# Low parts of the projection weights: an accumulating DMA in place of GpSimd's subtraction

## The chip, the cores and the metric

The kernel runs on one core of one Trainium2 chip. The metric is the device time of one execution in microseconds. Engines are named as the profile names them: PE (TensorE matmuls; PEld its weight loads), DVE (VectorE), ACT (ScalarE), POOL (GpSimd), SP (SyncE, which here only issues DMAs).

## What is computed

One block of a hybrid network over 2048 tokens of width 1024: a normalised and modulated input `h`, one large projection into 5960 columns, an RWKV-7 branch (a scan with state), an attention branch over the 256 best keys of each query, chosen by an index score, and a gated merge.

```python
h = rms_norm(x, norm_g[l]) * (1.0 + scale[:, None, :]) + shift[:, None, :]
p = h @ w_in[l]
...
y_a = rwkv7_branch(pr, pk, pv, pwd, pad_, w0[l], w2[l], a0[l], a2[l], k_k[l], k_a[l],
                   r_k[l], lnx_g[l], lnx_b[l])
y_b = dsa_branch(q, ckv, qi, ki, wi, kv_norm_g[l], w_uk[l], w_uv[l], rel_bias)
br_a = (y_a * jax.nn.silu(z_a)) @ w_pa[l]
br_b = (y_b * jax.nn.silu(z_b)) @ w_pb[l]
merged = jax.nn.sigmoid(g_a) * br_a + jax.nn.sigmoid(g_b) * br_b
x = x + gate[:, None, :] * (merged @ w_o[l])
```

The change is in `p = h @ w_in`.

## The kernel before

The projection is a GEMM in float32r with both operands split in two: a rounded high part (float32r) and what the rounding left, the low part. Each product takes three matmuls: weight high by `h` high, weight high by `h` low, weight low by `h` high, in this order for each of 8 slices of the contraction (L250 and L251). A *unit* is one block of 128 output columns for 512 tokens: 24 matmuls of 512 columns, or 48 of 256 (`self.cut`) in the second half. The tokens are four blocks of 512. First `gemm_index` makes five column blocks for all four token blocks; then `gemm_half` makes 42 column blocks for token blocks 0 and 1, and the same 42 for blocks 2 and 3. Between the halves, `h` of blocks 2 and 3 is loaded from DRAM into the same buffers. At this turn of the halves (the last two column blocks of the first, the first two of the second) a token block serves two column blocks in turn.

The weights of one column block are made in `weights_` (L228 to L238), 89 times: SP loads 512 KB into `wraw`, of which there is one buffer (`bufs=1`); ACT casts it into `whi`; POOL subtracts the two into `wlo`. `whi` and `wlo` have two buffers each. So the cast for a block waits for the load and for the matmuls of the block before last, and the next load waits for the subtraction. The first block has 72 columns; the rest of its 128 is set to zero.

After a unit, ACT and DVE take its result from PSUM (`evacuate`: tile `eo`, four buffers) and SP stores it. Around the GEMM run the selection (`select`: PE's index scores `ixs`, ACT's `re`, DVE's `sc`) and the RWKV passes. The order of instructions on each engine is fixed when the kernel is built: a scheduler plays the program through and takes what is ready, by priority; `weights` and `evacuate` run as `urgent`, ahead of all else. Each engine then takes its instructions in that order, SP's and POOL's DMAs too, and one that waits holds up those behind it.

Of the kernel before, what the change touches and what calls it, by code (L numbers as in the profile page):

```python
# [24 lines left out]
FT = mybir.dt.float32  # L25
FR = mybir.dt.float32r
BF = mybir.dt.bfloat16
I32 = mybir.dt.int32
AF = mybir.ActivationFunctionType
OP = mybir.AluOpType  # L30
# [10 lines left out]
TOPK = 256  # L41
# [4 lines left out]
# first columns of the projections  # L46
# [5 lines left out]
class Block:  # L52
# [19 lines left out]
    def move(self, dst, src, q=None):  # L72
        """a DMA of float32r words as they are"""
        f = [a.bitcast(FT) if a.dtype == FR else a for a in (dst, src)]
        return (q or self.nc.sync).dma_start(f[0], f[1])
# [4 lines left out]
    # ---------------------------------------------------------------- constants  # L80
    def consts(self):
# [6 lines left out]
        # scratch in DRAM  # L88
# [23 lines left out]
    # ---------------------------------------------------------------- start: modulation, norm, h^T  # L112
    def start(self):
# [59 lines left out]
        # the last third of the modulation is for the end  # L173
# [9 lines left out]
        # bias by distance; beyond the last bucket's start it is constant and drops out of the softmax  # L183
# [12 lines left out]
    def ada(self, w, cT, j, ahead):  # L196
        """a third of the modulation, partial sums by partition"""
# [15 lines left out]
    # ---------------------------------------------------------------- the projection GEMM  # L213
    @contextmanager
    def urgent(self):
        """what frees or feeds the tensor engine goes before all else"""
# [10 lines left out]
    def weights_(self, c0, n):  # L227
# [5 lines left out]
        if n < 128:  # L233
            nc.gpsimd.memset(hi.bitcast(FT), 0.0)
            nc.gpsimd.memset(lo.bitcast(FT), 0.0)
        nc.scalar.copy(hi[:, :, :n], raw[:, :, :n])  # L236
        nc.gpsimd.tensor_tensor(lo[:, :, :n], raw[:, :, :n], hi[:, :, :n].bitcast(FT), op=OP.subtract)  # L237
# [17 lines left out]
    def split_out(self, p, scale=None, rows=128):  # L255
        """FR hi and lo of a PSUM tile."""
# [44 lines left out]
    def gemm_half(self, tbs, kinds):  # L301
# [13 lines left out]
        # at the turn of the halves, a block of tokens serves two columns at a time  # L315
# [55 lines left out]
    # ---------------------------------------------------------------- index scores and the selection  # L371
    def select(self):
        """For each query the mask of its TOPK best keys (ties go to the lower index).

        A threshold is sought by the secant method on the count of scores at or above it, until the count is
        at most eight short of TOPK; the missing ones are then the largest below the threshold. Where the
        search has not ended so, a branch finds the TOPK-th largest value bit by bit.
        """
# [3 lines left out]
        with ExitStack() as ctx:  # L382
# [15 lines left out]
            for grp in self.groups:  # L398
# [9 lines left out]
                for g, qb in enumerate(grp):  # L408
# [20 lines left out]
                    # a first guess from mean and mean deviation of the keys that all rows see  # L429
# [10 lines left out]
                for it in range(self.passes):  # L440
                    if it:
                        # next threshold: a step of nothing once the count is near enough
# [15 lines left out]
                    for g, qb in enumerate(grp):  # L458
                        n = 128 * (qb + 1)
                        tg, cg = t[:, g:g + 1], cnt[:, g:g + 1]  # L460
                        if qb in self.on_act and it < self.passes - 1:
                            # with Sign a score equal to the threshold counts half: good enough to go on
# [5 lines left out]
                # rows that found their threshold  # L468
# [29 lines left out]
    def select_bits(self, grp, sc, hs, t, cnt, y, eq, w):  # L498
        """The selection for any scores: the TOPK-th largest value bit by bit, ties by prefix sums.

        Leaves 1 for the selected and 0 for the others as scores, and their threshold."""
# [24 lines left out]
    # ---------------------------------------------------------------- RWKV-7, chunks of 64  # L526
    def rwkv_open(self, ctx):
# [23 lines left out]
        # the small second factors: hi twice, and lo  # L551
# [48 lines left out]
    def parts(self, pool, t):  # L600
        """FR hi and lo of a tile"""
# [115 lines left out]
    def rwkv_inv(self, tb):  # L717
        """inverses of the unit triangular 32-blocks, one block a partition"""
# [23 lines left out]
    def rwkv_chain(self, tb):  # L742
# [8 lines left out]
        for c in range(8):  # L751
# [15 lines left out]
            # off-diagonal block of the inverse  # L767
# [51 lines left out]
    def chain_out(self, tb, half, yt, yvar):  # L819
        """group norm and bonus of half a block, with features on partitions"""  # L820
# [537 lines left out]
```

## Time and profile before

| | |
|---|---|
| median of 3 runs | 2606.8 us (2601.84 to 2608.03) |
| span of the profiled execution | 2605.7 us |
| PE busy | 2449.8 us (94%) |
| DVE busy | 1750.5 us (67%) |
| ACT busy | 1229.8 us (47%) |
| POOL busy | 868.2 us (33%) |
| projection matmuls (L251) | 6528 of PE's 16776 instructions |
| POOL's subtraction (L237) | 89 times, 216.9 us |
| ACT's cast (L236) | 89 times, 92.8 us |

The profile is of one execution, and its span of 2605.7 us is that execution's own time as far as the profile tells it. Busy shares are means over stages with different limits. A matmul's own duration is longer than the distance to the next one, since they are pipelined. A wait is put down to the semaphore that came last.

### The profile page before, as it was taken

To read this page: it belongs to the slowest core of one execution; us is meant where nothing else is said; L and a number is where in the kernel's file an instruction comes from. 1 tells how busy PE (TensorE), PEld (TensorE's weight loads), DVE (VectorE), ACT (ScalarE), POOL (GpSimd) and SP (SyncE) were. 2 spreads that over 40 slices of the span, in tenths; PEclk is the share of its full clock that TensorE was granted. 3 is DMA by queue.
4 is the path that set the end of the run, shared out by engine and by line. 5 is a ranking of instruction groups with operands and counts; after the bars stand their busy time and mean duration, and the time that the engine had idled before them with its cause. 6 is when DMAs were issued, how large, how long until landed. Compare 5 with 4: busy or idle time off the path is not lost. (4 is left out here: it accounts for less than half of the span.)

```text
span 2605.7 us, 45357 instructions
## 1 busy us (share of the span) xinstructions
PE 2449.8 (94%) x16776; PEld 2153.8 (83%) x16776; DVE 1750.5 (67%) x3509; ACT 1229.8 (47%) x2136; POOL 868.2 (33%) x707
## 2 busy tenths in 40 slices
PE   4899999989899999899999999999989999999998
PEld 3687777868677899689898888988978999988887
DVE  6615888798988355774956947533468888877443
ACT  4315636446344423324334233343367888865332
POOL 2311131241323333223233322131155545645342
PEclk9999999999999999899999999999999999999999
DMA  7754222522233756568677669977763334145442
GB/s 245 271 149 127 77 85 73 131 77 88 84 103 102 243 162 202 147 192 234 179 219 204 187 189 284 293 233 189 239 199 116 91 88 118 45 152 195 147 150 77
DMA packets 423499, 415.69 MB, mean 160 GB/s; under 512 B 80010, under 2 KB 339890, under 8 KB 418404
## 3 DMA queue, kind: packets, MB, share of 16 engines
q1 hardware_dynamic: 422692, 404.33, 51.7%
q0 software_dynamic: 576, 8.39, 0.8%
q8 instruction: 132, 2.16, 0.4%
q14 instruction: 99, 0.81, 0.1%
HBM read 254.04 MB, written 160.15 MB: 159 GB/s over the span
## 5 line engine op out<-in xcount | busy, mean ns | idle before, releaser
L251 PE MATMUL g<-hh,whi 128*128 128x256 f32 (+1 forms) x2176 | 726.9, 334 | 14.8 <-DVE eo L265 4.5
L251 PE MATMUL g<-hl,whi 128*128 128x256 f32 (+1 forms) x2176 | 722.5, 332 | 3.9 <-POOL hl L169 2.4
L251 PE MATMUL g<-hh,wlo 128*128 128x256 f32 (+1 forms) x2176 | 721.0, 331 | 1.2 <-POOL wlo L237 1.2
L251 PEld LDWEIGHTS g<-hh,whi 128*128 128x128 f32 x2176 | 421.4, 194 | 63.8 <-issue 5.7
L251 PEld LDWEIGHTS g<-hl,whi 128*128 128x128 f32 x2176 | 421.0, 193 | 47.6 <-issue 3.9
L251 PEld LDWEIGHTS g<-hh,wlo 128*128 128x128 f32 x2176 | 420.7, 193 | 42.7 <-issue 3.9
L237 POOL TENSOR_TENSOR wlo<-wraw,whi 128x1024 fp32r<-128x1024 f32 (+1 forms) x89 | 216.9, 2437 | 629.4 <-ACT whi L236 583.0
L421 ACT ACTIVATE re<-ixs 128x512 f32<-128x512 f32 (+3 forms) x304 | 158.9, 548 | 176.1 <-DVE sc L427 109.8
L427 DVE SCALAR_TENSOR_TENSOR sc<-re,wi,sc 128x512 f32<-128x512 f32 (+3 forms) x266 | 222.6, 842 | 21.7 <-ACT re L421 6.5
L236 ACT CAST whi<-wraw 128x1024 fp32r<-128x1024 f32 (+1 forms) x89 | 92.8, 1042 | 175.1 <-PE g L251 131.0
L957 PE MATMUL pt<-ident,lt 128*128 128x128 f32 x1088 | 168.2, 276 | 6.4 <-ACT tp L963 3.5
L947 ACT ACTIVATE lt<-lt,nm 128x128 f32<-128x128 f32 (+15 forms) x128 | 154.7, 1211 | 14.2 <-DVE nm L946 14.1
L943 DVE CUSTOM_DVE_ANT_0 lt<-lg,mask 128x512 f32<-128x512 f32 (+3 forms) x256 | 147.4, 590 | 15.9 <-PE lg L941 7.5
L974 PE MATMUL yv<-ph,vp 128*128 128x256 f32 (+1 forms) x576 | 151.5, 285 | 6.7 <-ACT yl L978 4.7
L968 DVE TENSOR_TENSOR pl<-pt,ph 128x512 fp32r<-128x512 f32 (+1 forms) x216 | 139.1, 657 | 25.7 <-ACT ph L967 24.6
L974 PE MATMUL yv<-pl,vp 128*128 128x256 f32 x576 | 152.4, 300 | 2.0 <-POOL pl L965 2.0
L418 PE MATMUL ixs<-kim,st 128*128 128x512 f32 (+3 forms) x304 | 117.3, 387 | 28.7 <-ACT re L421 24.8
L940 PE MATMUL lg<-m,sq 128*128 128x256 f32 (+3 forms) x384 | 137.2, 366 | 5.0 <-DVE cm L943 4.1
L957 PEld LDWEIGHTS pt<-ident,lt 128*128 128x128 f32 x1088 | 125.9, 141 | 15.6 <-ACT tp L963 4.5
L941 PE MATMUL lg<-m,sq 128*128 128x256 f32 (+3 forms) x384 | 127.4, 337 | 0.0
L733 DVE TENSOR_TENSOR prd<-tm,ln 128x1 f32<-128x1 f32 (+30 forms) x124 | 113.3, 914 | 20.5 <-DMA pk<-pj 14.6
L967 ACT CAST ph<-pt 128x512 fp32r<-128x512 f32 (+1 forms) x216 | 115.9, 565 | 19.7 <-PE pt L957 13.7
(347 smaller groups left out, 5391.4 us busy)
## 6 DMA issues: line engine op xcount, KB each, us to landing
wraw<-in_w_in_dram SPq DMA_DIRECT2D x88, 512.0 KB
gg<-eo SPq DMA_DIRECT2D x64, 256.0 KB
gmd<-gt SPq DMA_DIRECT2D x64, 256.0 KB
gmc<-gmd SPq DMA_DIRECT2D x32, 512.0 KB
g<-gg SPq DMA_DIRECT2D x64, 256.0 KB
m<-ks SPq DMA_DIRECT2D x32, 512.0 KB
pj<-eo SPq DMA_DIRECT2D x52, 256.0 KB
x<-in_ada_w_dram SPq DMA_DIRECT2D x24, 512.0 KB
```

The source lines that it names most:

```text
L237: nc.gpsimd.tensor_tensor(lo[:, :, :n], raw[:, :, :n], hi[:, :, :n].bitcast(FT), op=OP.subtract)
L251: T.matmul(p[:, s], a[:, k], b[:, k, s], start=n == 0, stop=n == 3 * KD - 1)
L418: T.matmul(p[:, :kn], st[:, h], M[0][:, k0:k0 + kn], start=True, stop=False)
L421: A.activation(r[:, :kn], p[:, :kn], AF.Relu)
L427: V.scalar_tensor_tensor(o, r[:, :kn], wi, o, op0=OP.mult, op1=OP.add)
L940: T.matmul(p[:, :kn], sq[:, qb * 128:(qb + 1) * 128], m1[:, k0:k1_], start=True, stop=False)
L941: T.matmul(p[:, :kn], sq[:, qb * 128:(qb + 1) * 128], m2[:, k0:k1_], start=False, stop=True)
L943: V.tensor_tensor_reduce(lt[:, k0:k1_], p[:, :kn], mk, 1.0, -3.0e38, OP.add, OP.max, cm[:, i:i + 1])
L947: ex = A.activation(lt[:, :n], lt[:, :n], AF.Exp, bias=nm, accum_out=lsum[:, qb, h:h + 1])
L957: T.transpose(p[:, o:o + 128], L[i][:, kt * 128:(kt + 1) * 128], self.ident)
L968: V.tensor_tensor(pl[:, :n], p[:, :n], ph[:, :n].bitcast(FT), op=OP.subtract)
L974: T.matmul(yv[:, qs], vp[:, kt, :], b[:, o:o + nn], start=kt == 0 and i == 0, stop=kt == last and i == 1, skip_group_check=True)
```

## The change

`weights_` makes the low part in another way. ACT casts the whole raw block into `whi` as before, and then writes the same cast with a factor of -1 into `wlo`. A DMA that POOL issues then adds the raw block onto `wlo`, inside SBUF. The zeros for the first block's missing columns are set in `wraw` and no longer in `whi` and `wlo`. The remaining lines of the diff take comments away. Behind these lines a line number of the new kernel is higher by one.

```diff
         hi = w.tile([128, KD, 128], FR, name="whi")
         lo = w.tile([128, KD, 128], FR, name="wlo")
         if n < 128:
-            nc.gpsimd.memset(hi.bitcast(FT), 0.0)
-            nc.gpsimd.memset(lo.bitcast(FT), 0.0)
-        nc.scalar.copy(hi[:, :, :n], raw[:, :, :n])
-        nc.gpsimd.tensor_tensor(lo[:, :, :n], raw[:, :, :n], hi[:, :, :n].bitcast(FT), op=OP.subtract)
+            nc.gpsimd.memset(raw[:, :, n:], 0.0)
+        nc.scalar.copy(hi, raw)
+
+        nc.scalar.activation(lo, raw, AF.Copy, scale=-1.0)
+        nc.gpsimd.dma_start(lo.bitcast(FT), raw, accum_op=OP.add)
         return hi, lo
```

The scheduler also orders the instructions anew. ACT before, in the middle of the first half (`whi` is the cast, `eo` a unit's evacuation, `ja` a count of the selection):

```order
L236 CAST whi<-wraw 128x1024
L347 COPY eo<-g 128x512
L464 ACTIVATE ja,cnt<-sc,t 128x1408
L347 COPY eo<-g 128x512
L464 ACTIVATE ja,cnt<-sc,t 128x1408
L236 CAST whi<-wraw 128x1024
L464 ACTIVATE ja,cnt<-sc,t 128x1408
L347 COPY eo<-g 128x512 x2
L236 CAST whi<-wraw 128x1024
```

ACT after, at the same place:

```order
L235 CAST whi<-wraw 128x1024
L348 COPY eo<-g 128x512
L237 ACTIVATE wlo<-wraw 128x1024
L348 COPY eo<-g 128x512
L235 CAST whi<-wraw 128x1024
L348 COPY eo<-g 128x512
L237 ACTIVATE wlo<-wraw 128x1024
L482 UNCONDITIONAL_BRANCH
```

The negation (L237) stands behind the evacuation that follows the cast, and not right behind the cast. It is so in most of the 89 blocks.

POOL before, from the first weight block on (`hl` is the low part of `h`, `hhs` and `hls` its store to DRAM):

```order
L234 MEMSET whi 128x1024
L235 MEMSET wlo 128x1024
L237 ISA
L237 TENSOR_TENSOR wlo<-wraw,whi 128x8x72
L237 TENSOR_TENSOR wlo<-wraw,whi 128x1024
L169 TENSOR_TENSOR hl<-h,hh 128x512 x15
L75 DMA hhs_64<-hh 128x4096
```

POOL after, from the same place:

```order
L234 MEMSET wraw 128x8x56
L238 DMA wlo<-wraw 128x1024
L169 ISA
L169 TENSOR_TENSOR hl<-h,hh 128x512 x2
L238 DMA wlo<-wraw 128x1024
L169 TENSOR_TENSOR hl<-h,hh 128x512 x13
L75 DMA hhs_64<-hh 128x4096
```

The second weight block's DMA stands behind two of the `hl` subtractions, where its subtraction stood ahead of them all; from there on the DMAs stand about where the subtractions stood.

## Rows read from the trace of the kernel before

**Rows 1.** Page, part 1: busy us (share of the span) and instructions of each engine.

```profile
PE 2449.8 (94%) x16776; PEld 2153.8 (83%) x16776; DVE 1750.5 (67%) x3509; ACT 1229.8 (47%) x2136; POOL 868.2 (33%) x707
```

**Rows 2.** Stretches in us: length, busy us of each engine, PE clock, DMA share, GB/s.

```profile
500.00:840.00 340.00, 315.62 (x1373) 253.45 (x1372) 294.55 (x610) 160.26 (x298) 98.25 (x31) 0.98 0.29 88
840.00:905.00 65.00, 61.54 (x414) 55.74 (x413) 23.57 (x49) 25.15 (x38) 26.84 (x25) 0.95 0.82 253
905.00:1050.00 145.00, 144.50 (x1118) 134.91 (x1116) 75.48 (x114) 46.76 (x70) 50.49 (x34) 1.00 0.61 180
1050.00:1400.00 350.00, 330.55 (x2986) 299.83 (x2987) 245.49 (x359) 127.24 (x205) 113.35 (x102) 0.97 0.69 198
```

**Rows 3.** Tile wraw, POOL's subtraction: count, ns min/median/max, first and last start, forms.

```profile
L237 POOL TENSOR_TENSOR wlo<-wraw,whi x89: 1397/2400/3267, 37.9 to 1708.0; 128x1024 fp32r<-128x1024 f32 x88, 128x576 fp32r<-128x576 f32 x1
```

**Rows 4.** POOL in order of time: start us, us, engine, line, op, idle before.

```profile
457.47 2.53 POOL L237 TENSOR_TENSOR wlo<-wraw,whi 128x1024 fp32r<-128x1024 f32 x1 [14.65 <-ACT whi L236]
469.50 2.39 POOL L237 TENSOR_TENSOR wlo<-wraw,whi 128x1024 fp32r<-128x1024 f32 x1 [9.49 <-ACT whi L236]
...
502.06 2.40 POOL L237 TENSOR_TENSOR wlo<-wraw,whi 128x1024 fp32r<-128x1024 f32 x1 [8.74 <-ACT whi L236]
512.68 2.39 POOL L237 TENSOR_TENSOR wlo<-wraw,whi 128x1024 fp32r<-128x1024 f32 x1 [8.22 <-ACT whi L236]
...
622.10 2.43 POOL L237 TENSOR_TENSOR wlo<-wraw,whi 128x1024 fp32r<-128x1024 f32 x1 [6.08 <-ACT whi L236]
...
643.86 2.39 POOL L237 TENSOR_TENSOR wlo<-wraw,whi 128x1024 fp32r<-128x1024 f32 x1 [8.49 <-ACT whi L236]
...
808.09 2.40 POOL L237 TENSOR_TENSOR wlo<-wraw,whi 128x1024 fp32r<-128x1024 f32 x1 [1.68 <-ACT whi L236]
...
830.10 2.39 POOL L237 TENSOR_TENSOR wlo<-wraw,whi 128x1024 fp32r<-128x1024 f32 x1 [8.50 <-ACT whi L236]
```

**Rows 5.** ACT in order of time, a dense run and a cast after the turn.

```profile
500.95 1.04 ACT L236 CAST whi<-wraw 128x1024 fp32r<-128x1024 f32 x1
501.89 0.57 ACT L347 COPY eo<-g 128x512 f32<-128x512 f32 x1
...
511.55 1.05 ACT L236 CAST whi<-wraw 128x1024 fp32r<-128x1024 f32 x1 [4.67 <-PE g L251]
...
897.44 1.05 ACT L236 CAST whi<-wraw 128x1024 fp32r<-128x1024 f32 x1 [1.54 <-DMA wraw<-in_w_in_dram]
```

**Rows 6.** SP's queue in order of time: two loads of the raw block.

```profile
504.49 0.38 SPq L230 DMA_DIRECT2D wraw<-in_w_in_dram  x1
...
893.35 0.38 SPq L230 DMA_DIRECT2D wraw<-in_w_in_dram  x1
```

**Rows 7.** DMA queue q0 (page, part 3), landing of hhs, and its issue on POOL.

```profile
q0 software_dynamic: 576, 8.39, 0.8%
...
DMA to landing us min/median/max: 9.3/9.7/10.0
...
98.60 0.78 POOL L75 DMA_DIRECT2D hhs<-hh  x1
```

**Rows 8.** POOL in order of time, the turn of the halves.

```profile
847.45 2.39 POOL L237 TENSOR_TENSOR wlo<-wraw,whi 128x1024 fp32r<-128x1024 f32 x1
...
880.20 2.38 POOL L237 TENSOR_TENSOR wlo<-wraw,whi 128x1024 fp32r<-128x1024 f32 x1
...
898.57 2.41 POOL L237 TENSOR_TENSOR wlo<-wraw,whi 128x1024 fp32r<-128x1024 f32 x1 [1.41 <-ACT whi L236]
```

**Rows 9.** PE's weight loads in order of time, inside the turn.

```profile
882.63 0.19 PEld L251 LDWEIGHTS g<-hh,wlo 128*128 128x128 f32 x1 [1.45 <-POOL wlo L237]
```

**Rows 10.** DVE in order of time, beside POOL's subtraction at 880.20.

```profile
880.33 2.27 DVE L336 SCALAR_TENSOR_TENSOR eo<-prev,mu,eo 128x1 f32<-128x1 f32 x1
```

**Rows 11.** PE's waits up to 1750: us in total, times, longest.

```profile
PE ixs L418 <- ACT re L421: 24.8, 15, 3.3
```

## The prediction

> **What bounds the kernel now.** First the busy shares of the page: PE is busy for 94% of the span and POOL, whose subtraction goes, for 33% [rows 1]. So time that POOL saves is worth nothing by itself; what counts is what PE waits for. Then the table of stretches, to find where PE has idle time that a change could take or give: 24.4 us in 500 to 840, 3.5 in the turn of the halves at 840 to 905, 0.5 in 905 to 1050 and 19.5 in 1050 to 1400 [rows 2]. The 89 weight blocks are made from 37.9 to 1708.0 [rows 3], so this is where the change can act. A microsecond that PE loses up to the turn will mostly stay in the time: the stretch behind it has no idle time to give back, and the next little.
>
> Third, the pace at which weights are used, from POOL's rows. The subtractions of one run start 10.8 us apart, five of them from 469.50 to 512.68, three from 622.10 to 643.86 and three from 808.09 to 830.10 [rows 4]: PE turns over a weight in 10.8 to 11.0 us where it does nothing else. Fourth, the path that makes the next weight. It has one raw buffer, and so it is a ring: cast, subtraction, load into the buffer just read, next cast. In the run, the cast starts at 500.95 and takes 1.04, the subtraction runs from 502.06 to 504.46, SP issues the load at 504.49, and the next cast starts at 511.55, released by PE and not by the load [rows 4 to 6]. The load is seen where a cast waited for it: issued at 893.35, cast at 897.44, so 4.1 us [rows 5, 6]. The ring before is thus 3.5 + 4.1 = 7.6 us where DMA is quiet, against 10.8 of PE. It has 3 us to spare, and the low part is ready at 504.46 for a weight that PE begins at about 511.6, when it frees the older buffer: 7.1 us early, and 7.5 to its first use, the third matmul.
>
> **The change part by part.** *POOL's subtraction (89 of 2.4 us) goes*, and 89 DMA issues come. A DMA instruction took POOL 0.78 us for 2 MB [rows 7]. It waits in the same place of POOL's queue, for the negation rather than for the cast; what stands behind it is let go 1.6 us later and held for 1.6 us less. I put that at nothing.
>
> *ACT's negation is added*: 128 x 1024 from f32 to fp32r, the form of the cast, 1.04 us, 89 times, 93 us. ACT is under half busy, and its other work goes on. But on the ring it counts, and the order shows that the evacuation of the last unit now stands between cast and negation (0.57 us, at 501.89 [rows 5]). The cast's next instruction starts 0.94 after it. So the accumulating DMA is issued 0.94 + 0.5 + 1.05 = 2.5 us after the cast starts, where the subtraction started at 1.1.
>
> *The accumulating DMA*, X from POOL's issue to the last byte. The trace has no such transfer. Lower end: the same 512 KB on SP's queue, 4.1 us. Upper end: the only transfers of POOL's queue, 2 MB in 9.7 us (median to landing) [rows 7]. The nearest row is this last, brought to size: q0 was busy for 0.8% of the span of all engines with four transfers, 0.008 x 2605.7 / 4 = 5.2 us each; a quarter of the bytes saves 3.9 and leaves 5.8. An add also reads the destination, which can cost up to a second 1.3 us: 7.1. That row was taken at a busy time, so I take X = 6.0, and keep 4.1 and 9.7 for the range.
> The Trainium skill, page "DMA: Bandwidth & Descriptors", section "Anatomy of one DMA — SWDGE (gpsimd) path", fits 2.0 us + bytes / 436e3. By it X would be an estimated 3.2 us and the sum some 10 us rather than 40. But by the same fit the 2 MB would take 6.8 us, and the row has 9.7; the measurement decides.
>
> *The ring with it*: 2.5 + 0.1 + 6.0 + 0.1 + 4.1 = 12.8 us, against 10.8 of PE. The low part is now ready 2.6 + 6.0 = 8.6 us after the cast, not 3.5: of the 7.5 us of lead 2.4 are left, and each further weight of a dense run loses 2.0.
> - Run 469 to 513: four links of 2.0 and one before of 0.7 (457.47 to 469.50, 12.0 apart), 8.7, less 2.4: **6 us**.
> - The runs of three at 622 and 808: two links each and one before them, 6, less 2.4, so 3.6 each. For shorter bunches of two I add 1: **8 us**.
> - The turn of the halves. Here two column blocks share the tokens, SP is full with the loads of h, and there is no lead: PE's weight load sat idle until the subtraction ended (1.45 us before 882.63 [rows 9]). From the block whose subtraction starts at 847.45 to that of 898.57, five in series [rows 8], every link grows by 2.6 + X - 3.5 = 5.1 us. That is 25, less 2 that the first has in hand: **24 us** (23.5). A raw load that waits on SP also holds the h loads behind it; this is inside that number.
> - The first block at the start: the low part comes some 6 us later, where the page's first slices are limited by DMA and DVE. 0 to 4; I take **2**.
> - Elsewhere **0**: blocks are 18.8 us apart on the mean (1670 us / 89 [rows 3]), PE does other work between, and a ring of 12.8 is hidden by it. Without that cover each would lose 2.0 like those of a run.
> - DVE: POOL's subtraction holds DVE's operand reads up. A one-element instruction took 2.27 us from 880.33 to 882.60, beside the subtraction of 880.20 to 882.58 [rows 8, 10]. That goes, and the selection may gain: PE sat idle 24.8 us for ACT's scores [rows 11], which come after DVE's. Against it stand 1.05 us of ACT more for each block in that stretch, about 25 of the 89 by the mean spacing. Gain at most 24.8, loss at most 26; I set them off at 0, since PE is the limit there for all but 24 of 340 us.
> - DMA share: 89 x 2 x 1.3 us of all engines, 9% of the span. Priced in X and the loads.
>
> Sum: 6 + 8 + 24 + 2 = 40 us. The profiled execution spans 2605.7, 1.1 under the median of 2606.8; 2605.7 + 40 + 1.1 = **2647 us**, 1.5% slower.
>
> **The rivals.**
> 1. *The transfer is short* (X up to 4.6). Ring 2.5 + 0.2 + 4.1 + 4.1 = 10.9, as long as PE's block: the dense runs lose nothing, and the turn loses 5 x 3.2 - 2 = 14. For it: the transfer stays inside the chip's SBUF. Against: the 9.7 us row. Time 2621.
> 2. *The transfer is long.* If descriptors come late or the add halves the rate, X = 8: ring 14.8, 4 us lost in each of the eleven links above, less three leads of 0.4: 42; turn 5 x 7.1 - 2 = 34; with the start and bunches that now come short, 10 more, 86 in all: 2693. At the upper end of 9.7 it would be over 2730. For it: DVE is busy for 295 of 340 us in the stretch where the dense runs lie [rows 2], and POOL and DVE do hold each other up [rows 8, 10].
> The Trainium skill, page "SBUF — State Buffer", section "Who interferes with whom", says that a DMA issued by GpSimd can be starved of descriptors while DVE holds the shared port. No row here shows it for a DMA: the four of POOL's queue are too few.
> 3. *Faster.* With POOL's subtraction gone, DVE's stalls beside it go, and the 24.8 us in which PE waited for scores come back [rows 11]. It needs X at 4.1, so that the runs lose nothing and the turn 14: 2606.8 + 14 - 25 = 2596. Its place is the selection, up to 840; it decides if PE's wait for scores there falls by more than the turn takes. For it: the 2.27 us row. Against: the selection's DVE work is between PE's own, and ACT gets 1 us a block more.
> 4. *Nothing to see*: PE's order is moved a little by the new code, and losses of 10 us are met by as much gain. 2607.
>
> **How the numbers follow.** Forecast (X from 5 to 7.3) 0.52; short 0.18; long 0.14; faster 0.10; nothing 0.06. A measurement of this kernel can tell about 0.3%, 8 us, from no change. Short lies between 2607 and 2625 and gives a sixth of its chance to "within"; so faster 0.10, same 0.09, slower 0.81. The range leaves out the faster case and most of the long one beyond X = 8.5: 2607 to 2705.
>
> **What would show it.** After the change: casts in the dense runs released by the load of the raw block and not by PE, and 12 to 13.5 us apart; PE idle for the accumulated low part, some 30 to 40 us where 1.2 were; the turn of the halves longer by 20 to 30 us; the time from 1050 on as before. A landing of the accumulating DMA under 4.6 us, or a wait of PE for it under 10 us, would prove the step of X wrong; an unchanged pace of 10.8 in the runs with X near 6, the ring.

## The result and the profile after

The kernel with the change takes 2624.4 us (median of 5 runs, 2619.57 to 2634.21) beside 2608.03 for the kernel before on the same chip (2601.84 to 2611.07): a ratio of 1.0068, 95% interval 1.0049 to 1.0087. It is slower by 18 us by this ratio (16 by the medians) where 40 were forecast. The profiled execution spans 2622.6 us, 16.9 more than that of before.

From the page: busy us; POOL's queue (packets, MB, share of 16 engines); the matmuls of the low part and the casts (busy us, mean ns, idle time before them and what ended most of it); the new transfer (us to landing):

```profile
PE 2448.9 (93%) x16776; PEld 2154.6 (82%) x16776; DVE 1652.0 (63%) x3509; ACT 1310.7 (50%) x2225; POOL 723.9 (28%) x706
...
q0 software_dynamic: 13392, 55.06, 10.2%
...
L252 PE MATMUL g<-hh,wlo 128*128 128x256 f32 (+1 forms) x2176 | 719.3, 331 | 9.3 <-DMA wlo<-wraw 9.3
...
L235 ACT CAST whi<-wraw 128x1024 fp32r<-128x1024 f32 x89 | 93.2, 1047 | 238.8 <-DMA wraw<-in_w_in_dram 153.4
...
wlo<-wraw POOLq DMA_DIRECT2D x89, 512.0 KB, 5.5
```

PE's work is the same; DVE does the same 3509 instructions in 98.5 us less [rows 1]. POOL's queue has grown from 0.8% [rows 7] to 10.2%, and its transfer lands 5.5 us after its issue, in the median. The same transfer by stretch (min/median/max us to landing; 300 to 820, 905 to 1400, 1400 to 1770):

```profile
DMA to landing us min/median/max: 4.5/4.6/6.5
...
DMA to landing us min/median/max: 4.5/6.2/8.4
...
DMA to landing us min/median/max: 5.0/8.4/10.0
```

X is thus no single number: 4.6 where the dense runs lie, 8.4 in the last stretch, where other transfers fill the DMA. The stretches of [rows 2] after the change:

```profile
500.00:840.00 340.00, 318.12 (x1395) 256.15 (x1394) 255.53 (x610) 183.93 (x324) 64.40 (x32) 0.98 0.51 133
840.00:905.00 65.00, 53.70 (x353) 49.26 (x354) 19.42 (x47) 25.55 (x37) 19.59 (x24) 0.89 0.78 229
905.00:1050.00 145.00, 145.00 (x1135) 135.95 (x1134) 67.66 (x116) 56.38 (x81) 34.11 (x32) 1.00 0.76 207
1050.00:1400.00 350.00, 325.71 (x2933) 295.31 (x2932) 227.12 (x352) 137.13 (x213) 92.51 (x102) 0.95 0.80 217
```

In 840 to 905 there are 11.3 us without PE work where there were 3.5, at a lower mean of the granted clock (0.89, a mix of its levels of 1.2 and 2.4 GHz; 0.95 before). PE now comes to the turn earlier, so these are not the same matmuls; those are counted next. In 500 to 840 DVE is busy for 256 us instead of 295.

**Where the time went.** PE's projection matmuls (6528 in both) can be counted in order of time, and their starts compared. No. 2497 is the first of the second half of the tokens: the turn. Before, it starts at 850.8; 192 matmuls (two weight blocks) later PE is at 881.0; the last starts at 1747.8. Differences to these, worked out from the start times of one profiled execution each; negative is ahead:

| kernel | turn, 850.8 | 881.0 | last, 1747.8 | span, 2605.7 |
|---|---|---|---|---|
| the change | -17.5 | +1.1 | +11.3 | +16.9 |

So the change is no uniform loss: PE comes to the turn 17.5 us early, loses 18.6 within two blocks, and loses 16 more behind them. At the first two marks PE has done the same work as before (but for 2 of some 3300 instructions at the turn); by the last it has done 24 instructions more. Four other kernels with the subtraction for blocks 0 to 43 (below) come there from 3.2 us ahead to 3.7 behind, so a lead is known to some 4 us. The gain ahead of the turn shows in the stretch from 60 to the turn, before and after (columns as in [rows 2]):

```profile
60.00:850.80 790.80, 741.18 (x3196) 592.67 (x3197) 599.92 (x1152) 367.49 (x631) 200.45 (x85) 0.97 0.38 115
```

```profile
60.00:833.30 773.30, 732.83 (x3191) 587.35 (x3191) 531.78 (x1133) 408.01 (x674) 121.45 (x77) 0.98 0.54 147
```

For the same work (some twenty DVE instructions fall on the other side of the cut) DVE is busy 68 us less; PE is idle 40.5 us instead of 49.6 and, at a better mean clock, busy 8.4 us less. In this execution half of the lead is waits and half shorter busy time. Only the first half comes back in others: from the start to the turn PE is idle for 84.4 to 90.1 us in the five kernels with the subtraction for blocks 0 to 43 and for 72.1 to 75.2 in the six with the adding DMA there, while the busy times overlap (763 to 768 and 758 to 765).

The ring in the dense run, POOL's issues, one of SP's raw loads, and the casts on either side of it:

```profile
489.99 0.86 POOL L238 DMA_DIRECT2D wlo<-wraw  x1 [11.11 <-ACT wlo L237]
501.65 0.86 POOL L238 DMA_DIRECT2D wlo<-wraw  x1 [10.80 <-ACT wlo L237]
513.26 0.86 POOL L238 DMA_DIRECT2D wlo<-wraw  x1 [10.75 <-ACT wlo L237]
```

```profile
506.19 0.38 SPq L230 DMA_DIRECT2D wraw<-in_w_in_dram  x1
```

```profile
498.86 1.05 ACT L235 CAST whi<-wraw 128x1024 fp32r<-128x1024 f32 x1 [3.73 <-DMA wraw<-in_w_in_dram]
...
510.48 1.05 ACT L235 CAST whi<-wraw 128x1024 fp32r<-128x1024 f32 x1 [6.88 <-DMA wraw<-in_w_in_dram]
```

Cast 498.86, issue 501.65 (2.8 later), raw load 506.19 (X = 4.5), cast 510.48 (4.3): 11.6 us for this block, with the cast released by the load and not by PE as in [rows 5]. Over the run, from the issue at 465.20 to that at 525.62, five blocks take 12.1 us each on the mean. The ring binds the casts, as forecast, but by some 1.3 us a block and not by 2.0. And PE loses nothing by it here: in 440 to 530 it is as busy as before, with seven blocks in both (before, after; columns as in [rows 2]):

```profile
440.00:530.00 90.00, 89.18 (x394) 71.66 (x392) 74.28 (x154) 42.84 (x65) 19.06 (x8) 1.00 0.43 115
```

```profile
440.00:530.00 90.00, 88.89 (x397) 72.11 (x396) 62.55 (x154) 48.65 (x71) 6.04 (x7) 1.00 0.62 152
```

The turn, on POOL, PE and SP:

```profile
830.55 0.85 POOL L238 DMA_DIRECT2D wlo<-wraw  x1 [14.58 <-DMA hh<-hhs]
```

```profile
840.23 0.58 PE L252 MATMUL g<-hh,wlo 128*128 128x256 f32 x1 [6.42 <-DMA wlo<-wraw]
```

```profile
842.27 0.38 SPq L230 DMA_DIRECT2D wraw<-in_w_in_dram  x1
...
864.93 1.86 SPq L230 DMA_DIRECT2D wraw<-in_w_in_dram  x1
```

The stretch 830 to 840:

```profile
830.00:840.00 10.00, 3.81 (x20) 2.99 (x18) 0.15 (x1) 0.84 (x2) 0.85 (x1) 0.86 1.02 294
```

PE reaches the second half and stops 6.42 us for the low part of its first block, issued at 830.55 into a DMA that the reload of `h` fills (share 1.02). Only when it has landed does SP load the next raw block (842.27), and the one after that follows 22.7 us later. The two blocks of the turn, before and after, and what PE waits for in them after the change (us in total, times, longest):

```profile
850.84:880.99 30.15, 27.94 (x194) 25.74 (x192) 6.68 (x17) 5.09 (x7) 8.84 (x9) 0.89 0.94 292
```

```profile
833.30:882.04 48.74, 32.41 (x195) 29.64 (x194) 12.09 (x36) 10.93 (x14) 11.83 (x17) 0.82 0.86 255
```

```profile
PE g L252 <- DMA wlo<-wraw: 6.4, 1, 6.4
PE g L252 <- DMA hl<-hls: 3.3, 5, 1.6
PE g L252 <- DVE eo L337: 2.4, 1, 2.4
PE g L252 <- DMA hh<-hhs: 2.4, 3, 1.4
```

So of the 18.6 us 14.1 are idle time (16.3 for 2.2), of which the stop for the low part is 6.4; the waits for the reload of `h` grow from 2.0 to 5.7, and one of SP's loads of `h` waits 7.0 us for PE (4.8 before). The other 4.5 us are busy time at a lower mean clock (0.82 for 0.89).

Behind the two blocks, from 882 to 1770, PE waits for no low part at all. Its longest wait there is for a cast of ACT that has nothing to do with the weights:

```profile
PE pg L632 <- ACT kk L604: 11.3, 2, 9.2
```

### The profile page after: what moved, and what is told of

Same layout as the page of the kernel before. It is cut to its first block, busy times and chain, and to the rows that moved or that the text cites. A ratio compares the mean times of both kernels' runs of the same rounds, so it can differ in the third digit from the quotient of the medians.

```text
span 2622.6 us, 45567 instructions
## 1 busy us (share of the span) xinstructions
PE 2448.9 (93%) x16776; PEld 2154.6 (82%) x16776; DVE 1652.0 (63%) x3509; ACT 1310.7 (50%) x2225; POOL 723.9 (28%) x706
## 3 DMA queue, kind: packets, MB, share of 16 engines
q0 software_dynamic: 13392, 55.06, 10.2%
## 4 chain that ended last, share of the span: by engine, by line
PE 48%; DMA 9%; DVE 8%; issue 4%; ACT 2%; SPq 2%; POOL 1%; POOLq 0%; DVEq 0%; ACTq 0%
PE g L252 15%; PE fo L1178 5%; PE br L1093 5%; PE yv L975 4%; PE pt L958 3%; PE lg L941 2%; PE lg L942 2%; PE pg L699 2%; DVE prd L734 2%; PE pp L785 1%; DVE tm L736 1%; PE pp L782 1%; PE zu L791 1%; PE pp L802 1%; DMA bo<-bod 1%
## 5 line engine op out<-in xcount | busy, mean ns | idle before, releaser
L252 PEld LDWEIGHTS g<-hh,wlo 128*128 128x128 f32 x2176 | 420.3, 193 | 50.7 <-DMA wlo<-wraw 10.2
L238 POOL DMA_DIRECT2D wlo<-wraw x89 | 79.1, 889 | 737.8 <-ACT wlo L237 646.2
L428 DVE SCALAR_TENSOR_TENSOR sc<-re,wi,sc 128x512 f32<-128x512 f32 (+3 forms) x266 | 206.6, 782 | 27.4 <-ACT re L422 11.8
L235 ACT CAST whi<-wraw 128x1024 fp32r<-128x1024 f32 x89 | 93.2, 1047 | 238.8 <-DMA wraw<-in_w_in_dram 153.4
L969 DVE TENSOR_TENSOR pl<-pt,ph 128x512 fp32r<-128x512 f32 (+1 forms) x216 | 138.9, 656 | 28.6 <-ACT ph L968 27.8
L975 PEld LDWEIGHTS yv<-ph,vp 128*128 128x128 f32 x576 | 109.3, 191 | 12.4 <-ACT yl L979 3.5
```

Of the source, the lines that this page charges most:

```text
L252: T.matmul(p[:, s], a[:, k], b[:, k, s], start=n == 0, stop=n == 3 * KD - 1)
L428: V.scalar_tensor_tensor(o, r[:, :kn], wi, o, op0=OP.mult, op1=OP.add)
L969: V.tensor_tensor(pl[:, :n], p[:, :n], ph[:, :n].bitcast(FT), op=OP.subtract)
L975: T.matmul(yv[:, qs], vp[:, kt, :], b[:, o:o + nn], start=kt == 0 and i == 0, stop=kt == last and i == 1, skip_group_check=True)
```

## The experiments

The weight blocks are numbered 0 to 88 in the order of `weights_`: 0 to 46 for the first half of the tokens, 47 on for the second; 47 and 48 are taken together. Ratios are to the kernel before on the same chip, with the 95% interval. One per mil is 2.6 us. A single profiled execution lay up to 10 us beside its kernel's median, so the times of the runs carry the verdicts and the traces only tell where.

My theory after the result (theory 1): (a) the lead is DVE's relief, since GpSimd's subtraction held it; (b) the turn takes it back; (c) behind the turn the added DMA load costs. The rival: leads and losses come from the order of the instructions, which the scheduler works out anew for any edit.

### Where the change acts

The change in one part, the subtraction in the others, by a counter in `weights_`:

```diff
+        b = self.nblk = getattr(self, "nblk", -1) + 1
+        if b < 44:
             nc.scalar.copy(hi, raw)
             nc.scalar.activation(lo, raw, AF.Copy, scale=-1.0)
             nc.gpsimd.dma_start(lo.bitcast(FT), raw, accum_op=OP.add)
+        else:
+            nc.scalar.copy(hi[:, :, :n], raw[:, :, :n])
+            nc.gpsimd.tensor_tensor(lo[:, :, :n], raw[:, :, :n], hi[:, :, :n].bitcast(FT), op=OP.subtract)
```

> The accumulating DMA for blocks 0 to 43 alone; from block 44 on (the turn of the halves and everything behind it) GpSimd subtracts as before. Theory 1 (the time before the turn is won because GpSimd's subtraction no longer holds VectorE in the selection; the turn and the added DMA load behind it give it back): TensorE reaches the turn about 17 us ahead of the kernel before and keeps it; 2608 - 17 = 2591, ratio 0.993 to 0.996. Theory 2 (gain and losses come from the scheduler's different order, which any edit changes): no link between the part that is kept and the sign, 2598 to 2618, and the lead at the turn isn't kept. The prediction's own sum: 6 + 8 + 2 = 16 slower, 2624.

Measured: 0.9997 (0.9979 to 1.0014). PE is 14.0 us ahead at the turn, as theory 1 says, and the time has nothing of it: 7.9 are left at 881.

The same with another condition, all blocks but those around the turn:

```diff
-        if b < 44:
+        if not 44 <= b < 52:
```

> The accumulating DMA for all blocks but 44 to 51, those around the turn of the halves, where GpSimd subtracts as before. Theory 1 (the turn's loss of 16 is the ring of accumulate and raw load on a full DMA): the lead of 17 is kept through the turn, the late loss of 12 to 16 stays: 2608 - 17 + 14 = 2605, ratio about 0.999. Rival (the turn's loss comes from the DMA load of the blocks ahead and behind, or from the order): 2620 to 2626, as the change.

Measured: 0.9975 (0.9957 to 0.9993), 2602.5 us beside 2611.1. Theory 1's time, and 24 us less than the change: eight blocks make that difference, or the other order that comes with them. The lead is not kept whole: of 12.9 us at the turn 6.6 are left at 881.

What lies behind the turn:

```diff
-        if b < 44:
+        if b >= 52:
```

> GpSimd subtracts up to block 51, the accumulating DMA from block 52 on. Theory 1 (late loss of 12 to 16 between 1580 and 1770 us from the added DMA load): no lead before the turn, no loss in it, 2608 + 14 = 2622, ratio 1.005. Rival (the late loss only comes with the earlier shifts, or from the order): 2605 to 2611.

Measured: 0.9978 (0.9957 to 0.9998). Theory 1 falls here: behind the turn the change alone costs nothing net. Set against the subtraction, it may still lose by the DMA and win as much by what goes; this run cannot tell the two apart.

The turn alone:

```diff
-        if b < 44:
+        if 44 <= b < 52:
```

> The accumulating DMA for blocks 44 to 51 alone, those around the turn of the halves; GpSimd subtracts everywhere else. Theory 1, in its second form (the change's whole loss is made at the turn, where the accumulating DMAs stand behind the reload of h on a full DMA): 2608 + 12 to 24, so ratio 1.005 to 1.009, and TensorE stops for block 47's low part at the first matmuls of the second half. Rival (the turn only loses because the blocks ahead of it, all by DMA, ran back to back and left no weight in stock): no loss, 2603 to 2612.

Measured: 1.0059 (1.0038 to 1.0080), 15 us slower. The turn alone makes most of the loss, and needs no blocks ahead of it to do so. Nor is it a matter of order up to there: PE's executed order is that of before up to instruction 3228, and the turn is at 3301. PE's waits there (820 to 905; us in total, times, longest):

```profile
PE g L259 <- DMA wlo<-wraw: 9.5, 2, 5.2
PE g L259 <- ACT whi L237: 5.5, 1, 5.5
```

Three blocks left out:

```diff
-        if b < 44:
+        if not 46 <= b < 49:
```

> The accumulating DMA for all blocks but 46, 47 and 48, whose low parts are made while the reload of h fills the DMA. Theory 1, second form: as with 44 to 51 left out, ratio 0.996 to 1.000, with no stop of TensorE for a low part at the turn. Rival (the later blocks of the turn, 49 to 51, lose as much, or the loss is the whole kernel's DMA load): halfway or more, 1.003 to 1.007.

Measured: 1.0001 (0.9985 to 1.0017). Subtracting for three blocks of 89 takes the loss away (with another order behind the turn). The first block of the second half, in the run with eight left out:

```profile
833.69 2.38 POOL L245 TENSOR_TENSOR wlo<-wraw,whi 128x1024 fp32r<-128x1024 f32 x1 [11.79 <-ACT whi L244]
```

It needs no DMA, takes 2.38 us as everywhere [rows 3], and is done at 836.07; in the change, where PE came to the turn 4.7 us earlier, the DMA issued at 830.55 was done at 840.2.

The back-to-back stretch ahead of the turn left out too:

```diff
-        if b < 44:
+        if not 39 <= b < 52:
```

> The adding DMA for all blocks but 39 to 51, so that GpSimd subtracts also in the stretch ahead of the turn where the ring ran back to back at 11 to 12.5 us a block. If that stretch costs: 3 to 8 faster than with 44 to 51 left out (0.9975), 0.994 to 0.997. If not: the same, 0.997 to 1.000.

Measured: 0.9985 (0.9967 to 1.0003), no different from 0.9975. That stretch of the ring costs nothing that can be told.

The control, on the kernel before:

```diff
+        un = w.tile([128, 1, 128], BF, name="unused", bufs=1)
+        nc.gpsimd.tensor_copy(un[:, 0, :16], raw[:, 0, :16])
         nc.gpsimd.tensor_tensor(lo[:, :, :n], raw[:, :, :n], hi[:, :, :n].bitcast(FT), op=OP.subtract)
```

> The kernel before with one small GpSimd copy more per weight block (16 columns into a tile that nobody reads, some 0.1 us each): it only disturbs the order that is worked out when the kernel is built. Theory 1: within 0.2% of before, 2603 to 2613. Rival (order alone moves the time by as much as the change did): more than 0.4% either way.

Measured: 1.0003 (0.9984 to 1.0023). But this is no test of the rival: in the two traces PE's 16776 instructions, DVE's 3509 and ACT's 2136 are the same, one after the other, in operation, tiles and shapes. The small copies stand in POOL's order and moved nothing else.

So the rival has to be judged by pairs whose executed order agrees. In these counts of PE's 16776 places (tiles without their buffer numbers), the change agrees with the four kernels below that copy where it adds (everywhere or in one stretch) in every place, and so do the other engines; the turn alone agrees so with its copy. The change with the unused subtraction agrees in 16657 places, with the kernel before in only 9106. The kernels above that mix DMA and subtraction have orders of their own, so their total times carry the order with them.

### What the adding costs

The DMA copies instead of adding; all else stays:

```diff
-        nc.gpsimd.dma_start(lo.bitcast(FT), raw, accum_op=OP.add)
+        nc.gpsimd.dma_start(lo.bitcast(FT), raw)
```

> The change with the DMA copying the raw weights onto the low parts instead of adding them, so the low parts are wrong and the rest is the same work: it shows what the adding costs. If the adding is free beside the copy, the DMA lands in the same 5.5 us (median) and the time is that of the change, 2620 to 2630. If the adding is what takes the time, it lands 1.5 us or more earlier and the time is 2605 to 2618.

Measured: 2593.4 us in one run, less than either case expected. More runs of the same kernel:

> The copy in place of the adding once more (low parts wrong, the rest the same work), now timed. The first look gave 2593 beside 2608 and a DMA that lands in 3.9 us instead of 5.5. Theory 1, third form (the 1.6 us that the adding takes on each DMA decide the sign): ratio 0.993 to 0.997. Rival (the look was a lucky run, the cost is in the ring itself): 1.003 to 1.008.

Measured: 0.9954 (0.9936 to 0.9971). The order of the instructions is the same as the change's on all five engines, row for row, so this pair is clean: the adding costs 1.0068 - 0.9954, 30 us. Its page, and the tile's landing:

```profile
q0 software_dynamic: 13392, 55.06, 5.5%
...
wlo<-wraw POOLq DMA_DIRECT2D x89, 512.0 KB, 3.5
```

The queue's share less the 0.8% of its other transfers is 4.7%, against 9.4% with the adding: adding took the DMA engines twice the time of copying (1.37 and 2.77 us each per transfer: share x span / 89). In the dense run POOL issues at the pace of PE again, 10.8 us apart on the mean of five blocks, of which these three are the closest:

```profile
484.38 0.53 POOL L239 DMA_DIRECT2D wlo<-wraw  x1 [10.34 <-ACT wlo L238]
494.44 0.53 POOL L239 DMA_DIRECT2D wlo<-wraw  x1 [9.53 <-ACT wlo L238]
504.62 0.53 POOL L239 DMA_DIRECT2D wlo<-wraw  x1 [9.65 <-ACT wlo L238]
```

In the stretch 300 to 820 the copy lands in 2.9 us where the adding takes 4.6. The Trainium skill's fit that the prediction weighed (page "DMA: Bandwidth & Descriptors", section "Anatomy of one DMA — SWDGE (gpsimd) path") gives an estimated 3.2 for these bytes: the trace agrees for the copy where DMA is quiet, and has half as much again for the adding.

The copy in the kernel with the DMA at the turn alone; its order is that of the adding there:

```diff
             nc.scalar.activation(lo, raw, AF.Copy, scale=-1.0)
-            nc.gpsimd.dma_start(lo.bitcast(FT), raw, accum_op=OP.add)
+            nc.gpsimd.dma_start(lo.bitcast(FT), raw)
```

> The copy in place of the adding for blocks 44 to 51 alone (their low parts wrong), GpSimd subtracting everywhere else; to be set beside the adding there, 1.0059. If the adding is what costs at the turn: a third of it or less is left, ratio 0.999 to 1.002. Rival (the full DMA and the raw block that is held are what costs at the turn, whatever the DMA does with the data): 1.004 to 1.007.

Measured: 1.0040 (1.0020 to 1.0061), against 1.0059. Two thirds of the turn's loss stay by these numbers, though the intervals overlap. In the run with the copy everywhere, the turn's first low part, PE's stop for it and the next raw load:

```profile
821.21 0.53 POOL L239 DMA_DIRECT2D wlo<-wraw  x1 [14.51 <-DMA hh<-hhs]
```

```profile
829.26 0.58 PE L259 MATMUL g<-hh,wlo 128*128 128x256 f32 x1 [4.79 <-DMA wlo<-wraw]
```

```profile
832.24 0.38 SPq L230 DMA_DIRECT2D wraw<-in_w_in_dram  x1
```

Here the copy takes 8.0 us to land where the adding took 9.6, each 5 more than in the dense run: on a full DMA the 1.6 us between them are the smaller part. The next raw load follows its issue by 11.0 us, with the adding by 11.7; up to 3 us of this it stands behind reloads of `h` in SP's order.

The copy in one stretch of the change and the adding in the others, again with the change's own order (and `44 <= b < 52`, `b >= 52` for the other two):

```diff
+        if b < 44:
+            nc.gpsimd.dma_start(lo.bitcast(FT), raw)
+        else:
             nc.gpsimd.dma_start(lo.bitcast(FT), raw, accum_op=OP.add)
```

> The change with the copy in place of the adding for blocks 0 to 43 alone (low parts wrong there), same order on every engine. Theory P (the adding's time is paid wherever the ring binds; from the two traces 10 in the first half, 2 at the turn, 20 behind it): 10 of the 30 gone, ratio 1.002 to 1.004. Rival Q (the first half's gain is lost again at the turn, where the reload of h waits for nothing but the DMA): 1.005 to 1.008, as the change.

Measured: 1.0013 (0.9995 to 1.0031), 14 us less than the change.

> The same with the copy for blocks 44 to 51 alone. Theory P: 2 to 5 gone, ratio 1.005 to 1.006. Rival Q (the turn decides): 15 or more gone, below 1.001.

Measured: 1.0027 (1.0014 to 1.0041), 11 us less.

> The same with the copy from block 52 on. Theory P: 20 gone, ratio 0.998 to 1.000. Rival Q: nothing gone, 1.005 to 1.008.

Measured: 0.9983 (0.9966 to 1.0000), 22 us less.

Theory P holds behind the turn and, within the interval, for the first half; at the turn neither does (11 us, where P had 2 to 5 and Q 15 or more). The parts add up to 47, the whole is 30; each difference is uncertain by some 7, and that a microsecond saved in two places is paid once is likely but not shown. Behind the turn the adding costs 22 us against the copy, and nothing against the subtraction (0.9978 above): two different comparisons, the first in one order, the second in two.

### What the missing subtraction is worth

The change with a subtraction that nobody reads:

```diff
         nc.gpsimd.dma_start(lo.bitcast(FT), raw, accum_op=OP.add)
+        if b < 44:
+            un = w.tile([128, 1, 128], BF, name="unused", bufs=1)
+            for k in range(KD):
+                nc.gpsimd.tensor_tensor(un, raw[:, k:k + 1], hi[:, k:k + 1].bitcast(FT), op=OP.subtract)
```

> The change, and for blocks 0 to 43 GpSimd also subtracts into a tile that nobody reads (8 pieces of 128 columns, in bf16), so that it works beside VectorE again. Theory 1 (GpSimd's subtraction slowed VectorE in the selection): the lead of 17 at the turn is gone: 2624 + 17 = 2641, ratio to before about 1.013, and VectorE's busy time between 120 and 840 us is back by most of the 65 us that the change saved there. Rival (the lead comes from the order, or from GpSimd's own release times): 2620 to 2628, and the lead stays.

Measured: 1.0099 (1.0069 to 1.0129), and a lead of 5.8 at the turn in place of 17.5, with PE's order the same in all but 119 places and POOL's issues in the dense run no further apart (486.70, 498.51, 509.47). Theory 1 in direction, smaller in size: DVE's busy time from 60 us to the turn is 555.5, where it was 599.9 before and 531.8 with the change, so a third of the saving is back:

```profile
60.00:845.00 785.00, 741.33 (x3192) 591.50 (x3191) 555.46 (x1136) 409.61 (x674) 306.09 (x413) 0.97 0.53 145
```

That narrow pieces hold DVE less would explain this, but was not tested. The rise in the time by itself, 1.0099 over 1.0068, is within the intervals. The selection's costliest DVE group, before, after, and with the unused subtraction (count | busy, mean ns | idle before):

```profile
L427 DVE SCALAR_TENSOR_TENSOR sc<-re,wi,sc 128x512 f32<-128x512 f32 (+3 forms) x266 | 222.6, 842 | 21.7 <-ACT re L421 6.5
```

```profile
L428 DVE SCALAR_TENSOR_TENSOR sc<-re,wi,sc 128x512 f32<-128x512 f32 (+3 forms) x266 | 206.6, 782 | 27.4 <-ACT re L422 11.8
```

```profile
L439 DVE SCALAR_TENSOR_TENSOR sc<-re,wi,sc 128x512 f32<-128x512 f32 (+3 forms) x266 | 214.8, 813 | 22.8 <-ACT re L433 6.7
```

842 ns, 782, and 813 with GpSimd subtracting into nothing. This does not hang on the order: in all five kernels with the subtraction up to block 43 the mean is 842 or 849 ns, and in the fourteen executions with a DMA or the negation alone up to block 38 at least it is 782 to 802. The Trainium skill, page "SBUF — State Buffer", section "Who interferes with whom", states that a VectorE instruction with two inputs in SBUF contends with a GpSimd instruction that reads SBUF; these three rows agree with it.

Now the negation alone, no DMA and no subtraction, first for blocks 0 to 43 (with the subtraction behind them) and then for all:

```diff
-            nc.gpsimd.dma_start(lo.bitcast(FT), raw, accum_op=OP.add)
```

> Blocks 0 to 43 with the negation alone, no DMA and no subtraction (their low parts wrong), GpSimd subtracting from 44 on: VectorE's relief without the ring. Beside it stands the same split with the adding DMA, 0.9997. Theory A (the ring of the first half costs the 10 to 16 that the prediction gave it, and the relief pays for it): 10 to 16 faster than that, ratio 0.993 to 0.996. Theory B (the ring costs next to nothing there; the lead at the turn is lost at the turn, which is held by the reload of h and by GpSimd): 0.998 to 1.001.

Measured: 0.9988 (0.9970 to 1.0006): theory B's time. The lead is 26.9 at the turn, 13 more than with the DMA, and the time has nothing of that.

> All blocks with the negation alone, no DMA and no subtraction (low parts wrong): VectorE's relief and ScalarE's extra work without the ring. Theory P (the ring's price goes on falling with the time between negation and reload): faster than the copy (0.9954) by as much again per us, 10 or more, 0.985 to 0.992. Rival (at the copy's 3.9 us the ring is already off the path): 0.993 to 0.997.

Measured: 0.9830 (0.9807 to 0.9852), 44 us faster than before. Without subtraction, and with nothing in its place but ACT's negation, that much is to be had; the change stands 62 above it, the copy 32. The page, and the stretch 840 to 905, where PE now works 63.2 of 65 us at the full clock (here the two blocks of the turn end at 852):

```profile
PE 2438.7 (95%) x16776; PEld 2152.0 (84%) x16776; DVE 1637.3 (64%) x3509; ACT 1308.0 (51%) x2221; POOL 641.9 (25%) x617
```

```profile
840.00:905.00 65.00, 63.20 (x505) 60.82 (x504) 28.07 (x52) 34.22 (x49) 13.64 (x14) 1.00 0.58 167
```

### The ring, or the late low part

The DMA adds from the weights in DRAM, so that the raw block is free after the negation:

```diff
-        nc.gpsimd.dma_start(lo.bitcast(FT), raw, accum_op=OP.add)
+        src = self.x["w_in"][:, c0:c0 + n].rearrange("(k p) m -> p k m", p=128)
+        nc.gpsimd.dma_start(lo[:, :, :n], src.bitcast(FR), accum_op=OP.add)
```

> The change with the DMA adding the weights straight from DRAM, so that the raw block is free after the negation; 46 MB more are read from DRAM. If the ring (the raw block held until the DMA lands) is what costs: most of the 62 us between the change and the negation alone come back, ratio 0.984 to 0.995. If the late low part, or the DMA load, is what costs: 1.000 to 1.010 or more; the pieces of 512 bytes, eight times as many, may make each DMA longer still.

Measured: 1.0106 (1.0067 to 1.0145), slower than the change. Casts wait 33.7 us in all for raw loads where they waited 153.4, so the ring is mostly open; but the transfer is longer and PE waits for it:

```profile
q0 software_dynamic: 93136, 54.83, 15.3%
...
wlo<-in_w_in_dram POOLq DMA_DIRECT2D x88, 512.0 KB, 8.8
```

```profile
PE g L253 <- DMA wlo<-in_w_in_dram: 31.6, 13, 9.5
```

And the same with GpSimd's subtraction around the turn:

```diff
+        if not 44 <= b < 52:
             nc.gpsimd.dma_start(lo[:, :, :n], src.bitcast(FR), accum_op=OP.add)
+        else:
+            nc.gpsimd.tensor_tensor(lo[:, :, :n], raw[:, :, :n], hi[:, :, :n].bitcast(FT), op=OP.subtract)
```

> The same, but GpSimd subtracts for blocks 44 to 51. If the turn still loses by low parts that land late in the reload of h: 5 to 15 faster than with all blocks from DRAM. If the ring was the turn's cost too: within 0.2% of it, or slower by what GpSimd's subtraction costs there.

Measured: 1.0078 (1.0053 to 1.0103), 7 us less, within both intervals. By PE's wait of 31.6 us, where the change had 9.3, a late low part costs by itself; how the 62 divide between it and the ring isn't separated by these two, because X grew from 5.5 to 8.8 as the ring went.

### All leads in one table

| first half (blocks 0 to 43) | executions | lead at the turn, us | mean |
|---|---|---|---|
| subtraction | before and four others | -3.7 to 3.2 | -1.3 |
| adding DMA | the change and five others | 12.9 to 17.7 | 15.4 |
| copying DMA | three | 21.5 to 26.9 | 23.6 |
| negation alone | two | 26.9, 27.8 | 27.4 |
| adding DMA and unused subtraction | one | 5.8 | |
| adding DMA from DRAM | two | 3.0, 5.6 | 4.3 |

| blocks 47 and 48 at the turn | executions | lost in 192 matmuls, us |
|---|---|---|
| adding or copying DMA inside SBUF | nine | 16.8 to 22.3 |
| adding DMA from DRAM | one | 12.5 |
| subtraction on GpSimd | eight, without before | -0.3 to 6.8 |
| negation alone | one | -1.1 |

Subtraction, adding inside SBUF and negation alone do not overlap in the first table, nor the DMA inside SBUF and the subtraction in the second. The copy and the negation do, and two executions of the copy lie 4.6 apart. So ahead of the turn negation alone is 27 us ahead of the kernel before, of which the adding DMA takes 12; what the copy takes cannot be told from the scatter. The turn takes some 19 with either DMA inside SBUF. Between rows of the first table the order differs too; with the order almost the same, the unused subtraction moved the lead by 12.

## Why the prediction was wrong

The sign was right and the sum more than twice too large: 40 forecast, 18 measured. Of the prediction's own signs, one came: the casts of the dense run are released by the raw load (11.2 to 12.4 us apart, where 12 to 13.5 were named). PE's wait for the low part, forecast at 30 to 40 us, is 9.3 in all, of which 2.9 lie ahead of the turn. Under 10 was to prove the step of X wrong; X itself lands near its 6.0, so what fails is the step from X to PE's wait. The turn is longer by 18.6, where 20 to 30 were named, and the time from 1050 on is not as before. By its steps:

- **DVE's relief, set off at 0 against ACT's negation: the step that failed.** The gain is 27 us by the turn (negation alone), and 44 over the kernel with nothing in the subtraction's place. That DVE is held by the subtraction is shown by its instruction of 842 ns, 782 without; of the lead, 12 us went with the unused subtraction in almost the same order. That all of the 27 and 44 is DVE's relief is not shown: those two kernels have another order, and no transfer or subtraction that their low parts wait for. The prediction had the mechanism in its row of 2.27 us, and priced it only by PE's wait for scores, at most 24.8, less an ACT instruction of 1.05 us per block at full price. Neither held: that wait fell only from 24.8 [rows 11] to 17.0, the rest came mostly from other waits; and ACT's price is already inside the 44 us, which have all 89 negations in them. Rival 3, given 0.10, named this mechanism, and expected it to decide the sign.
- **X taken as one number, 6.0.** As a mean it was near (median 5.5). But it is 4.6 in the stretch of the dense runs, where 6.0 was charged, 9.6 at the turn's first block, and 8.4 in the last stretch, where nothing was charged. Rival 1's short transfer was thus true in one place and false in the others; that its 2621 is close to the result is an accident of two errors. The adding was allowed "up to a second 1.3 us"; it measured 1.4 more engine time per transfer (2.77 against 1.37).
- **The dense runs and the start, 6 + 8 + 2 = 16.** The ring came out at 12.1 in the dense run, not 12.8, and it held up the casts but not PE, which was as busy there as before. By the table the first half does lose 12 to the adding DMA. That this is near 16 is luck: the 12 us do not lie where the sum put them, and where they lie was not found.
- **The turn, 24.** Right in place and nearly in size: 18.6 in the trace, 15 us alone, 24 by leaving eight blocks out. Its mechanism was partly other than told: not five equal links, but the first blocks of the second half, whose transfer meets the reload of `h`; 6.4 us are the stop itself, and the rest follows it (more waiting for the reload, a lower clock).
- **Elsewhere, 0.** Wrong: in the trace 15.8 us go between 881 and the end, and the copy behind the turn alone gives 22 back. The cover that the prediction named, 18.8 us from block to block, is a mean; with X at 6.2 and 8.4 on a busier DMA (share 0.80 in 1050 to 1400, 0.69 before) the casts do wait for raw loads (153.4 us in all, 33.0 before). But PE waits for no low part there, and its longest wait, 9.2 us for `kk`, stands also in the trace with the copy behind the turn. So by which way the loss reaches PE is not shown.

By the trace's own sum: 17.5 gained ahead of the turn (27 of relief less 10 for the DMA, by the kernel with the negation alone), 18.6 lost at the turn and 15.8 behind it, which is the 16.9 of the spans. The forecast had 16 + 24 + 0 of losses and no gain. The relief at 0 made it too large, the 0 elsewhere too small, and the two partly cancel.

**What stays open.** Why a lead at the turn is worth so little at the end where GpSimd subtracts or the DMA adds behind it (the first-half kernels lead by 8 and 20 at 881 and end level in the runs), and by which wait the adding costs its 22 us behind the turn. The rival of the order is not excluded for the totals of the kernels that mix DMA and subtraction, nor for the 44 us of the negation alone: the control left the order as it was, so how much an order by itself can move was never measured. Also open is how the 62 us divide between ring and late low part.

The version with the subtraction kept for blocks 44 to 51 beats both kernels, at 0.9975, though by less than the 0.3% that one measurement tells.

## What to carry to other kernels

Before you set a gain and a loss off at nothing, price each alone: here 44 us stood against 62, and the difference told little of either. A transfer's time belongs to the place where it is waited for, so take it by stretch, and look first where a bulk reload fills the DMA: with the subtraction for three blocks of 89 the loss was gone. An accumulating DMA that holds its source buffer is a link of that buffer's ring; test it with a plain copy, which leaves the order of the program as it is.

## What was not expected of the hardware

- An accumulating DMA inside SBUF, 512 KB, took the engines twice the time of the same copy (2.77 and 1.37 us per transfer), landed in 4.6 us instead of 2.9 where DMA is quiet, and held POOL 0.86 us for the issue instead of 0.53.
- Adding from DRAM in pieces of 512 bytes landed in 8.8 us in the median, where the add from SBUF took 5.5.
- DVE's instructions of two inputs in SBUF (128x512 f32) took 842 or 849 ns on the mean in the five kernels where GpSimd subtracted for the first 44 blocks and 782 to 802 where it did not, in whatever order the kernel ran.
